# An encoder layer on one core: where the bias lines are drawn, and how the norm's gain g reaches all partitions

## The chip, the cores and the metric

The kernel runs on one core of a Trainium2 chip. A core has five engines with a queue of instructions each: TensorE (PE in the profile, with its weight loads as PEld), VectorE (DVE), ScalarE (ACT), GpSimd (POOL) and SyncE (SP). They run side by side and meet through semaphores; transfers between device memory and the on-chip buffer are issued from the queues of SP, ACT and POOL and run on 16 shared DMA engines. The metric is the device time of one execution in microseconds, as the median of three runs.

## The reference

An encoder layer on two inputs, a prompt of 256 rows and a sample of 1024 rows, both 1024 wide. Every row is normalised and scaled by a gain, projected, run through two kinds of banded attention, gated, added back, and put through a squared-ReLU MLP. What the change touches is the first norm and the attention's bias:

```python
def _rmsnorm(x, g):
    y = x32 * lax.rsqrt(jnp.mean(x32 * x32, axis=-1, keepdims=True) + RMS_EPS)
    return (y * g.astype(jnp.float32)).astype(x.dtype)
...
    h = _rmsnorm(x, g_mix)
    z = h @ w_in
...
    bias = bias_table.astype(jnp.float32)[_rel_bucket(rel * dist_scale)]
    logits = jnp.where(valid[None, :, None, None], s + bias, NEG_INF)
```

The bias of a head depends on the distance of key and query alone, so that all of it is in one line for each head and each spacing. There are 20 heads and 2048 positions in all such lines together.

## The kernel before

The ten row tiles (128 rows each, eight of the sample and two of the prompt, called tiles 0 to 9 here) stay on chip. Matrix products are made in three TensorE passes on operands that are split into a high and a low part (`hhi`/`hlo` of the rows, `vhi`/`vlo` of weights); later stages use a fast matrix product of seven block products. The order of the first stage is written by hand: each engine's instructions stand in its queue in the order in which the code is written, and every engine takes them strictly from its own queue.

The first stage makes the transposed normalised rows and the value projection. Its steps:

- `load_x(t)` brings tile t, `load_v(v, i)` a piece of the value weights (`vraw`), all on SP's queue. SP also issues `tab` (the bias table), `bg` (the gate's bias, a rearranged load of single elements) and `nsink`, and before the change `gm`, the gain g broadcast from device memory to 128 partitions.
- `square(t)` is ACT's: the sum of squares of tile t, and its square root. `scale(t)` is DVE's: the reciprocal, and tile x reciprocal x `gm` into `xn`.
- `turn(t)` is in steps: eight TensorE transposes of `xn` (tile `tr`), then four copies on ACT to `hhi` and four subtractions on DVE to `hlo`.
- `split_v` makes `vhi` on ACT and `vlo` on DVE (one of four on POOL).
- `values(t, v, ps)` is 24 matmuls of 512 (or 384) columns: the value projection of tile t. `evac` copies it out and stores it.
- `warm(n)` are n matmuls of the identity with itself in fp32, whose result nobody reads; they stand ahead of and between the first transposes.
- `draw(i)` makes 512 positions of all bias lines: a matmul of the one-hot matrix `hot` (33 rows: 32 buckets and one for "outside the window") with the table `tab`, which is split into `tab_hi` and `tab_lo`, so two matmuls; ACT copies the result and POOL stores it to `scr_l`. The four draws stand behind the value projections of tiles 3 to 6. Each needs `hot` rounded to `hr` by POOL, and POOL also issues that load.

A word on transfers. Each transfer adds 16 to one of eight counters when it has landed (for SP and ACT together they are named DMAHW0 to DMAHW7). The counters are given out in turn, in the order in which the kernel's text issues transfers, and a transfer that takes a counter waits in its engine's queue until the one that had it before has landed.

Of the kernel before, what the change touches and what calls it, by code (L numbers as in the profile page):

```python
# [10 lines left out]
F32 = mybir.dt.float32  # L11
F32R = mybir.dt.float32r
AF = mybir.ActivationFunctionType
ALU = mybir.AluOpType

P = 128
D = 1024
# [6 lines left out]
AH = 8  # L24
BH = 4
FF = 4 * D
EPS = 1e-6
NEG = -1e30
BUCKETS, MAXD = 32, 1024
# [68 lines left out]
def encoder_kernel(  # L98
# [5 lines left out]
    nc = tc.nc  # L104
    PSUM = bass.MemoryType.PSUM

    def x_rows(t):
        return x_sample[0, P * t : P * (t + 1), :] if t < 8 else x_prompt[0, P * (t - 8) : P * (t - 7), :]
# [11 lines left out]
    const = ctx.enter_context(tc.tile_pool(name="const", bufs=1))  # L120
# [6 lines left out]
    def slot(name, shape=(P, D), dt=F32):  # L127
        return slots.tile(list(shape), dt, name=name, tag="m", bufs=N_M)
# [7 lines left out]
    def bank(tag, name=None):  # L136
        return psum.tile([P, 512], F32, name=name or tag, tag=tag, bufs={"mm": 3, "sc": 2, "pt": 2, "pv": 1}[tag])
# [111 lines left out]
    nc.vector.memset(eps, EPS)  # L249
    bg = const.tile([P, 2 * KC], F32, name="bg")  # L250
    nsink = const.tile([P, AH], F32, name="nsink")
    tab = const.tile([BUCKETS + 1, AH + 3 * BH], F32, name="tab")
    tab_hi, tab_lo = (const.tile([BUCKETS + 1, AH + 3 * BH], F32R, name=x) for x in ("tab_hi", "tab_lo"))

    nm_b = const.tile([P, ROWS], F32, name="nm_b")
    l_b = const.tile([P, ROWS], F32, name="l_b")
# [19 lines left out]
    NH = AH + 3 * BH  # L276
# [16 lines left out]
    NL = sum(x[5] for x in LINES)  # L293
    scr_l = dram.tile([NH, NL], F32, name="scr_l")
# [378 lines left out]
    with ExitStack() as pre:  # L673
        late = pre.enter_context(tc.tile_pool(name="values", bufs=1))

        def own(name, shape, dt=F32, n=1):
            return late.tile(list(shape), dt, name=name, tag=name, bufs=n)

        xs, sds = {}, {}
        gm = slot("gm")  # L680
# [3 lines left out]
        def load_x(t):  # L684
            xs[t] = slot("xt")
            nc.sync.dma_start(xs[t], x_rows(t))
# [11 lines left out]
        def split_v(v, i, eng=nc.vector):  # L698
            if v == 0:
                hi, lo = wslot("vhi", (P, 2, 512), F32R), wslot("vlo", (P, 2, 512), F32R)  # L700
            else:
                hi, lo = own("v2", (P, 2, 384), F32R, 8), own("v2", (P, 2, 384), F32R, 8)
            src = v_raw.pop((v, i))
            nc.scalar.activation(hi, src, AF.Copy)
            eng.tensor_tensor(lo, src, hi.bitcast(F32), op=ALU.subtract)
            v_parts[v, i] = hi, lo

        def warm(n):
            ps = bank("mm", "warm")
            for _ in range(n):  # L710
                nc.tensor.matmul(ps[:, :P], ident, ident, start=True, stop=True, skip_group_check=True)

        hots = {}

        def load_hot(i):
            if i < NL // 512:
                hs = own("hs", (P, 512))[: BUCKETS + 1, :]
                nc.gpsimd.dma_start(hs, hot[:, 512 * i : 512 * i + 512])
                hots[i] = own("hr", (P, 512), F32R)[: BUCKETS + 1, :]
                nc.gpsimd.tensor_copy(hots[i], hs)  # L720

        def draw(i):

            ps = bank("pv", "line")
            hs = hots.pop(i)
            for k, x in enumerate((tab_lo, tab_hi)):
                nc.tensor.matmul(ps[:NH, :], x, hs, start=not k, stop=k == 1)
            ln = own("vo", (P, 512), n=2)[:NH, :]
            nc.scalar.activation(ln, ps[:NH, :], AF.Copy)
            nc.gpsimd.dma_start(scr_l[:, 512 * i : 512 * i + 512], ln)  # L730
            load_hot(i + 1)

        def square(t):
            xn[t] = slot("xn")
            ss = small.tile([P, 1], F32, name="ss")
            nc.scalar.activation(xn[t], xs[t], AF.Square, accum_out=ss)
            sds[t] = small.tile([P, 1], F32, name="sd")
            nc.scalar.activation(sds[t], ss, AF.Sqrt, bias=eps, scale=1.0 / D)

        def scale(t):  # L740
            rs = small.tile([P, 1], F32, name="rs")
            nc.vector.reciprocal(rs, sds.pop(t))
            nc.vector.scalar_tensor_tensor(xn[t], xs.pop(t), rs, gm, op0=ALU.mult, op1=ALU.mult)
# [48 lines left out]
        def values(t, v, ps, ks=range(KC)):  # L792
            n = NV[v]
            for k in ks:
                lh, ll = h_at(k, P * t, P)
                rh, rl = (x[:, k % 2, :] for x in v_parts[v, k // 2])
                for j, (a, b) in enumerate(((lh, rh), (lh, rl), (ll, rh))):
                    nc.tensor.matmul(ps[:, :n], a, b, start=k == 0 and j == 0, stop=k == KC - 1 and j == 2)

        def evac(t, v, ps):  # L800
            rows = slice(P * t, P * t + P)
            vo = own("vo", (P, 512), n=2)[:, : NV[v]]
            if v == 0:
                nc.vector.tensor_copy(vo, ps)
            else:
                nc.scalar.activation(vo, ps[:, : NV[v]], AF.Copy)
            nc.gpsimd.dma_start(scr_v[rows, 512 * v : 512 * v + NV[v]], vo)

        load_x(0)
        nc.sync.dma_start(gm, g_mix[0].partition_broadcast(P))  # L810
        load_x(1)
        for i in range(4):
            load_v(0, i)
        for t in range(2, 6):
            load_x(t)
        nc.sync.dma_start(tab[:BUCKETS, :], rel_bias)
        nc.sync.dma_start(bg, b_gate[0].rearrange("(k p) -> p k", p=P))
        nc.sync.dma_start(nsink, sink[0].partition_broadcast(P))
        load_v(1, 0)
# [6 lines left out]
        load_x(9)  # L826
        first = small.tile([P, 1], F32, name="sd")
        nc.scalar.activation(first, eps, AF.Sqrt)
        warm(15)

        turns = [turn(t) for t in range(NT)]
        square(0)
        scale(0)
        next(turns[0])
        warm(4)
        square(1)
        scale(1)
        next(turns[0])
        split_v(0, 0)
        next(turns[1])  # L840
        warm(2)
        split_v(0, 1)
        next(turns[1])
        split_v(0, 2, nc.gpsimd)
# [12 lines left out]
        next(turns[1], None)  # L857
        square(4)
        next(turns[2], None)
        nc.vector.memset(tab[BUCKETS:, :], NEG)  # L860
        nc.vector.tensor_copy(tab_hi, tab)
        nc.vector.tensor_tensor(tab_lo, tab, tab_hi.bitcast(F32), op=ALU.subtract)
        load_hot(0)
        nc.vector.tensor_scalar(nsink, nsink, -1.0, None, op0=ALU.mult)
        for t in range(2):
            evac(t, 0, pss[t])
# [2 lines left out]
        for t in range(2, NT):  # L869
            if t + 1 < NT:  # L870
                next(turns[t + 1])
                next(turns[t + 1])
            if t + 3 < NT:
                square(t + 3)
            if t + 2 < NT:
                scale(t + 2)
            if t + 1 < NT:
                next(turns[t + 1], None)
            if t < 6:
                split_v(1, t - 2)  # L880
            if t > 7:
                next(b0)
            ps = bank("mm", "v")
            values(t, 0, ps)
            if 3 <= t < 3 + NL // 512:
                draw(t - 3)
            evac(t, 0, ps)

        def more():
# [14 lines left out]
        for t in (4, 5, 6, 7, 8, 9, 0, 1, 2, 3):  # L904
            ps = bank("mm", "v")
# [6 lines left out]
    if True:  # L912
# [16 lines left out]
        class Rows:  # L929
# [15 lines left out]
            def sum(self, t0, n, ps, other):  # L945
                out, a, b = self.views(t0, n, ps, other)
                nc.vector.scalar_tensor_tensor(out, a, self.scale, b, op0=ALU.mult, op1=ALU.add)
# [401 lines left out]
    if True:  # L1349
# [54 lines left out]
        n = len(order)  # L1404
# [87 lines left out]
        for i, (x, b, c) in enumerate(jobs):  # L1492
            t0, n = BLOCKS[b]
# [15 lines left out]
            ps = bank("mm")  # L1509
# [79 lines left out]
    with ExitStack() as pre:  # L1589
# [7 lines left out]
        gm = slot("gm2")  # L1597
# [12 lines left out]
        for hh in range(2):  # L1610
# [17 lines left out]
            for t in range(NT):  # L1628
                m = parts.pop(t)
                ps = bank("mm")  # L1630
# [391 lines left out]
```

## Time and profile before

| | us |
|---|---|
| median of three runs | 1682.21 (1681.28 to 1682.70) |
| the profiled execution | 1681.33 |
| its span on the core | 1679.5 |
| TensorE busy in the span | 1667.2 (99%) |
| VectorE, ScalarE, GpSimd busy | 951.4, 718.2, 512.1 |

The span is the time between the first and the last instruction on the core; 1.8 us of the profiled execution lie around it. Rows of the timeline begin with the start and the duration in us; where a group of equal instructions is merged, "x8" tells how many. Behind "<-" stand in brackets the idle time of the engine just before, and what ended it. TensorE's rows overlap each other, since a matmul starts before the one ahead of it has drained; so its steps are read from start to start. A plain fp32 matmul leaves two records.

### The profile page before, as it was taken

Reading aid. Unit: us, or ns where it says so; the run is one execution under the profiler, and the core shown is the slowest. Engines: PE = TensorE matmul, PEld = TensorE weight load, DVE = VectorE, ACT = ScalarE, POOL = GpSimd, SP = SyncE. Lnnn points to the kernel's source line nnn. Section 1 sums busy time; section 2 is a strip of 40 time slices with the busy share of each in tenths; the row PEclk is TensorE's granted clock in tenths of the full one; section 3 lists DMA queues with packets and bytes.
Section 4 is the critical chain, followed back from the end, with each engine's and each line's share of the span. In section 5 each row is a group of like instructions: output and inputs, shape, how many; then the busy total and the mean of one; then the engine's idle time right before and its main releaser. Section 6 shows DMA issues by size and latency. Waiting matters only on the chain. (4 is left out here: it accounts for less than half of the span.)

```text
span 1679.5 us, 24942 instructions
## 1 busy us (share of the span) xinstructions
PE 1667.2 (99%) x9268; PEld 1414.5 (84%) x9268; DVE 951.4 (57%) x1544; ACT 718.2 (43%) x1485; POOL 512.1 (30%) x404
## 2 busy tenths in 40 slices
PE   9999999999999999999999999999999999999998
PEld 7898888887788888888888888888888888888886
DVE  6732233455563566677278445545556775867665
ACT  6332323356662556654176333333334333333445
POOL 1312222122111463200100556556454250514240
PEclk9999999999999999999999999999999999999999
DMA  7426562567676793845121443443356934733333
GB/s 249 151 58 127 133 133 76 162 192 197 192 198 188 184 262 119 296 133 201 38 88 59 160 156 109 136 160 115 125 190 227 363 105 131 256 102 116 120 119 125
DMA packets 225881, 262.45 MB, mean 156 GB/s; under 512 B 30017, under 2 KB 154737, under 8 KB 225761
## 3 DMA queue, kind: packets, MB, share of 16 engines
q1 hardware_dynamic: 217536, 239.80, 44.8%
q0 software_dynamic: 7936, 20.54, 5.6%
q8 instruction: 73, 1.20, 0.3%
q10 hardware_dynamic: 288, 0.52, 0.1%
q14 instruction: 48, 0.39, 0.1%
HBM read 175.13 MB, written 90.92 MB: 158 GB/s over the span
## 5 line engine op out<-in xcount | busy, mean ns | idle before, releaser
L347 PE MATMUL dn<-dhi,ulo 128*128 128x512 f32 x448 | 174.5, 389 | 0.2
L347 PE MATMUL dn<-dlo,uhi 128*128 128x512 f32 x448 | 174.3, 389 | 0.0
L347 PE MATMUL dn<-dhi,uhi 128*128 128x512 f32 x448 | 174.3, 389 | 0.0
L347 PE MATMUL x<-chi,wlo 128*128 128x512 f32 x424 | 167.0, 394 | 0.1
L347 PE MATMUL x<-clo,whi 128*128 128x512 f32 x424 | 165.7, 391 | 0.1
L347 PE MATMUL x<-chi,whi 128*128 128x512 f32 x424 | 165.1, 389 | 0.0
L314 DVE TENSOR_TENSOR wlo<-ta,whi 128x1024 fp32r<-128x1024 f32 x30 | 55.2, 1841 | 173.8 <-ACT whi L312 173.8
L314 DVE TENSOR_TENSOR wlo<-raw,whi 128x1024 fp32r<-128x1024 f32 x60 | 89.0, 1483 | 98.1 <-ACT whi L312 96.5
L393 POOL TENSOR_TENSOR tb<-raw 128x512 f32<-128x512 f32 x25 | 32.5, 1298 | 366.8 <-DMA raw<-in_w_in_dram 146.5
L347 PEld LDWEIGHTS dn<-dhi,ulo 128*128 128x128 f32 x448 | 84.1, 188 | 18.4 <-PE dn L347 0.5
L347 PEld LDWEIGHTS dn<-dlo,uhi 128*128 128x128 f32 x448 | 84.1, 188 | 17.5
L347 PEld LDWEIGHTS dn<-dhi,uhi 128*128 128x128 f32 x448 | 84.1, 188 | 17.4
L347 PEld LDWEIGHTS x<-chi,whi 128*128 128x128 f32 x424 | 79.6, 188 | 17.0
L347 PEld LDWEIGHTS x<-chi,wlo 128*128 128x128 f32 x424 | 79.8, 188 | 15.7 <-ACT c L1936 0.6
L347 PEld LDWEIGHTS x<-clo,whi 128*128 128x128 f32 x424 | 79.8, 188 | 14.9 <-DVE clo L314 0.4
L1716 POOL TENSOR_TENSOR t<-raw,t 128x1024 f32<-128x1024 f32 x16 | 45.0, 2828 | 154.3 <-DMA raw<-in_w_down_dram 154.3
L186 DVE TENSOR_TENSOR ulo<-uraw,uhi 128x1024 fp32r<-128x1024 f32 x56 | 88.7, 1606 | 3.5 <-ACT uhi L185 3.5
L1865 DVE TENSOR_TENSOR v<-v,dn 128x512 f32<-128x512 f32 x90 | 59.4, 682 | 41.2 <-PE dn L347 36.6
L1965 POOL TENSOR_TENSOR u<-u,u 128x640 f32<-128x640 f32 x16 | 25.1, 1570 | 171.7 <-ACT u L1883 171.7
L186 DVE TENSOR_TENSOR dlo<-raw,dhi 128x1024 fp32r<-128x1024 f32 x32 | 48.6, 1540 | 47.2 <-ACT dhi L185 46.3
L347 PE MATMUL dn<-dhi,up 128*128 128x512 f32 x224 | 73.5, 389 | 0.0
L185 ACT ACTIVATE dhi<-raw 128x1024 fp32r<-128x1024 f32 x32 | 33.5, 1058 | 93.5 <-PE dn L347 93.0
(325 smaller groups left out, 4690.6 us busy)
## 6 DMA issues: line engine op xcount, KB each, us to landing
scr_u<-u SPq DMA_DIRECT2D x112, 320.0 KB, 2.6
uraw<-scr_u SPq DMA_DIRECT2D x56, 512.0 KB, 4.5
raw<-in_w_down_dram SPq DMA_DIRECT2D x36, 512.0 KB, 6.2
raw<-in_w_up_dram SPq DMA_DIRECT2D x32, 512.0 KB, 5.4
raw<-in_w_in_dram SPq DMA_DIRECT2D x25, 512.0 KB, 5.4
sg<-scr_g SPq DMA_DIRECT2D x32, 256.0 KB, 6.3
uraw<-scr_u SPq DMA_DIRECT2D x28, 256.0 KB, 4.3
v<-scr_v SPq DMA_DIRECT2D x96, 64.0 KB, 2.8
```

What stands on the lines that cost most here:

```text
L185: nc.scalar.activation(hi, src, AF.Copy)
L186: nc.vector.tensor_tensor(lo, src, hi.bitcast(F32), op=ALU.subtract)
L314: nc.vector.tensor_tensor(lo, src, hi.bitcast(F32), op=ALU.subtract)
L347: nc.tensor.matmul(ps, a, b, start=first and i == 0, stop=last and i == len(seq) - 1, skip_group_check=True)
L393: (nc.vector if vector else nc.gpsimd).tensor_tensor(o, x, y, op=ALU.subtract)
L1716: nc.gpsimd.tensor_tensor(o, a, b, op=ALU.subtract)
L1865: nc.vector.tensor_tensor(v, v, ps, op=ALU.add)
L1965: nc.gpsimd.tensor_tensor(u[S1], u21, u22, op=ALU.add)
```

## The change

Two things are moved, and one is added.

1. `gm` isn't broadcast by a transfer any more. SP's first transfer brings g as one row of 4 KB (`g_row`), TensorE multiplies it by a row of ones (two fp32 matmuls of 512 columns, ahead of the last `warm`), and DVE copies the two results to `gm`.
2. The bias lines are drawn in plain fp32 and in one accumulation: `tab` is a table padded with zeros in which draw j is shifted by 32 columns, so that the four draws fill rows 0, 32, 64 and 96 of one PSUM bank. Draw 0 stands between the transposes of tiles 0 and 1, draws 1 to 3 behind those of tile 1, in the place of `warm(4)` and `warm(2)`. The eight matmuls behind tiles 3 to 6 go, as do the split of the table on DVE, the rounding of `hot` on POOL and its loads there. One copy of the whole bank on ACT stands behind the values of tile 3, with four stores.
3. `tab` and the two halves of `hot` (33 rows of 1024 numbers, 132 KB each) are issued from ACT's queue: `tab` first of all, `hot` between the `square` of tile 0 and that of tile 1.

```diff
+        pads = NL // 512
+        edge = 32 * (pads - 1)
+        tab = own("tab", (P, edge + P))[: BUCKETS + 1, :]
+        nc.vector.memset(tab, 0.0)
+        nc.vector.memset(tab[BUCKETS:, edge : edge + NH], NEG)
+        nc.scalar.dma_start(tab[:BUCKETS, edge : edge + NH], rel_bias)
+        hots = []
+        drawn = bank("pv", "line")
...
+            hots.append(slot("hot")[: BUCKETS + 1, :])
+            nc.scalar.dma_start(hots[i], hot[:, D * i : D * i + D])
+
+        def draw(j):
+
+            nc.tensor.matmul(drawn, tab[:, edge - 32 * j : edge - 32 * j + P],
+                             hots[j // 2][:, 512 * (j % 2) : 512 * (j % 2) + 512], start=not j, stop=j == pads - 1)
+
+        def store_lines():
+
+            ln = own("vo", (P, 512), n=2)
+            nc.scalar.activation(ln, drawn, AF.Copy)
+            for j in range(pads):
+                nc.gpsimd.dma_start(scr_l[:, 512 * j : 512 * j + 512], ln[32 * j : 32 * j + NH, :])
...
+        ones = own("ones", (P, P))[:1, :]
+        nc.vector.memset(ones, 1.0)
+        g_row = slot("g_row")[:1, :]
+        nc.sync.dma_start(g_row, g_mix)
         load_x(0)
-        nc.sync.dma_start(gm, g_mix[0].partition_broadcast(P))
         load_x(1)
...
         for t in range(2, 6):
             load_x(t)
-        nc.sync.dma_start(tab[:BUCKETS, :], rel_bias)
         nc.sync.dma_start(bg, b_gate[0].rearrange("(k p) -> p k", p=P))
...
-        warm(15)
+        warm(8)
+        for h in range(2):
+            ps = bank("mm", "g")
+            nc.tensor.matmul(ps, ones, g_row[:, 512 * h : 512 * h + 512], start=True, stop=True)
+            nc.vector.tensor_copy(gm[:, 512 * h : 512 * h + 512], ps)
+        warm(10)
 
         turns = [turn(t) for t in range(NT)]
         square(0)
+        load_hot(0)
+        load_hot(1)
         scale(0)
         next(turns[0])
-        warm(4)
+        draw(0)
         square(1)
         scale(1)
         next(turns[0])
         split_v(0, 0)
         next(turns[1])
-        warm(2)
+        for j in (1, 2, 3):
+            draw(j)
...
-            if 3 <= t < 3 + NL // 512:
-                draw(t - 3)
+            if t == 3:
+                store_lines()
             evac(t, 0, ps)
```

In the order of the built program, ACT's queue from its start stood so before (the names are those above; what an instruction waits for stands in brackets, where DMAHW0 to 7 are the counters of transfers):

```order
L828 ACT_TABLE_LOAD
L828 ACTIVATE sd<-eps 128x1 [waits DVE_49]
L736 ACTIVATE xn,ss<-xt 128x1024 [waits DMAHW0_49]
L738 ACTIVATE sd<-ss,eps 128x1 [waits Activation_49]
L736 ACTIVATE xn,ss<-xt 128x1024 [waits DMAHW2_49]
L738 ACTIVATE sd<-ss,eps 128x1 [waits Activation_49]
L769 ACTIVATE hhi<-tr 128x2x128 [waits PE_49]
```

and now:

```order
L716 DMA tab<-in_rel_bias_dram 32x20 [waits DVE_49]
L833 ACT_TABLE_LOAD
L833 ACTIVATE sd<-eps 128x1
L739 ACTIVATE xn,ss<-xt 128x1024 [waits DMAHW2_49]
L741 ACTIVATE sd<-ss,eps 128x1 [waits Activation_49]
L722 DMA hot<-in_hot_dram 33x1024 [waits DMAHW2_49]
L722 DMA hot<-in_hot_dram 33x1024 [waits DMAHW3_49]
L739 ACTIVATE xn,ss<-xt 128x1024
L741 ACTIVATE sd<-ss,eps 128x1 [waits Activation_49]
L772 ACTIVATE hhi<-tr 128x2x128 [waits PE_49]
```

Three issues of transfers stand in ACT's queue that weren't there, two of them ahead of tile 1's square, and each of these two waits for a counter. Which transfers had these counters before is seen on SP's queue, which now stands so from the first transfer to tile 7 (the last two `xt` rows are tiles 6 and 7):

```order
L815 DMA g_row<-in_g_mix_dram 1x1024
L684 DMA xt<-in_x_sample_dram 128x1024 x2
L691 DMA vraw<-in_w_in_dram 128x2x512 x4
L684 DMA xt<-in_x_sample_dram 128x1024 [waits DMAHW0_49]
L684 DMA xt<-in_x_sample_dram 128x1024 [waits DMAHW1_49]
L684 DMA xt<-in_x_sample_dram 128x1024 [waits DMAHW2_49]
L684 DMA xt<-in_x_sample_dram 128x1024 [waits DMAHW3_49]
L822 DMA bg<-in_b_gate_dram 128x16x1 [waits DMAHW4_49]
...
L684 DMA xt<-in_x_sample_dram 128x1024 [waits DMAHW2_49]
L684 DMA xt<-in_x_sample_dram 128x1024 [waits DMAHW3_49]
```

So counter 2 is taken by tile 0, then by tile 4, then by tile 6; counter 3 by tiles 1, 5 and 7. In the kernel's text `load_hot` is called behind `load_x(9)`, and the two halves of `hot` are the next on counters 2 and 3: their waits are for a count of 48, three landed transfers.

On TensorE's queue the start stood so before:

```order
L711 MATMUL warm<-ident 128x128 x15
L338 MATMUL tr<-ident,xn 128x128 x8
L711 MATMUL warm<-ident 128x128 x4
L338 MATMUL tr<-ident,xn 128x128 x8
L711 MATMUL warm<-ident 128x128 x2
L798 MATMUL v<-vhi,hhi 128x512
```

and now:

```order
L709 MATMUL warm<-ident 128x128 x8
L837 MATMUL g<-g_row,ones 128x512 x2
L709 MATMUL warm<-ident 128x128 x10
L336 MATMUL tr<-ident,xn 128x128 x8
L726 MATMUL line<-hot,tab 128x512
L336 MATMUL tr<-ident,xn 128x128 x8
L726 MATMUL line<-hot,tab 128x512 x3
L801 MATMUL v<-vhi,hhi 128x512
```

The four draws stand ahead of the first matmul of the value projection, and the first of them ahead of tile 1's transposes.

More of the change, by code (lines that the diff above doesn't have):

```diff
@@ L251, in encoder_kernel @@
     nsink = const.tile([P, AH], F32, name="nsink")
-    tab = const.tile([BUCKETS + 1, AH + 3 * BH], F32, name="tab")
-    tab_hi, tab_lo = (const.tile([BUCKETS + 1, AH + 3 * BH], F32R, name=x) for x in ("tab_hi", "tab_lo"))
     nm_b = const.tile([P, ROWS], F32, name="nm_b")
@@ L711, in warm @@
                 nc.tensor.matmul(ps[:, :P], ident, ident, start=True, stop=True, skip_group_check=True)
-        hots = {}
-        def load_hot(i):
[L716 to L731, printed above, removed]
+        pads = NL // 512
[6 more added lines that the diff above has]
+        drawn = bank("pv", "line")
+        def load_hot(i):
+            hots.append(slot("hot")[: BUCKETS + 1, :])
[8 more added lines that the diff above has]
+                nc.gpsimd.dma_start(scr_l[:, 512 * j : 512 * j + 512], ln[32 * j : 32 * j + NH, :])
         def square(t):
@@ L859, in encoder_kernel @@
         next(turns[2], None)
[L860 to L863, printed above, removed]
         nc.vector.tensor_scalar(nsink, nsink, -1.0, None, op0=ALU.mult)
```

## The prediction

> **What bounds the kernel now.** I read the page first, then who TensorE waits for, then the timeline of the first 60 us, the transfers of that stretch, and the order of the built program. The page says which engine sets the time:
>
> ```profile
> span 1679.5 us, 24942 instructions
> PE 1667.2 (99%) x9268; PEld 1414.5 (84%) x9268; DVE 951.4 (57%) x1544; ACT 718.2 (43%) x1485; POOL 512.1 (30%) x404
> ```
>
> A busy TensorE could still be a stalled one, so the waits are needed; these are all that the view of TensorE's waits has:
>
> ```profile
> PE warm L711 <- POOL ident masks.py:199: 1.4, 1, 1.4
> PE tr L338 <- DVE xn L743: 1.2, 2, 0.9
> PE sc L1146 <- DVE m L1148: 1.0, 2, 0.7
> PE v L798 <- DVE vlo L705: 0.7, 1, 0.7
> PE sc L541 <- DMA qk<-scr_kb: 0.5, 1, 0.5
> PE mm L192 <- ACT z L999: 0.2, 1, 0.2
> ```
>
> Five microseconds in all, of which those on `ident`, `xn` and `vlo` belong to the start. From then on TensorE is a solid row of matmuls to the tail. So two things count: when the solid row starts, and how many steps are in it. Whatever delays its start delays the end by as much, for nothing later has slack to give it back. The start, on three engines:
>
> ```profile
> 7.87 1.06 ACT L736 ACTIVATE xn<-xt 128x1024 f32<-128x1024 f32 x1 [1.60 <-DMA xt<-in_x_sample_dram]
> ...
> 9.57 1.28 DVE L743 SCALAR_TENSOR_TENSOR xn<-xt,rs,gm 128x1024 f32<-128x1024 f32 x1
> ...
> 10.91 1.09 PE L338 MATMUL tr<-ident,xn 128*128 128x128 f32 x8 [0.92 <-DVE xn L743]
> ...
> 12.21 0.48 PE L798 MATMUL v<-vhi,hhi 128*128 128x512 f32 x1
> ...
> 13.37 0.50 PE L798 MATMUL v<-vlo,hhi 128*128 128x512 f32 x1 [0.68 <-DVE vlo L705]
> ```
>
> Tile 1's square starts when tile 1 lands (7.87). Its transposes follow 3.04 us later, and the second value matmul, from which the row is solid, 5.50 us later. One matmul was done ahead of it; with steps of 0.23 us the solid row starts, in effect, at 13.14.
>
> **Part 1: the draws leave the solid row.** A seam between two tiles without a draw, and one with:
>
> ```profile
> 31.15 0.40 PE L798 MATMUL v<-vhi,hlo 128*128 128x512 f32 x1
> 31.39 1.04 PE L338 MATMUL tr<-ident,xn 128*128 128x128 f32 x8
> 32.18 0.48 PE L798 MATMUL v<-vhi,hhi 128*128 128x512 f32 x1
> ...
> 37.49 0.39 PE L798 MATMUL v<-vhi,hlo 128*128 128x512 f32 x1
> 37.81 0.41 PE L727 MATMUL line<-hr,tab_lo 33*20 33x512 f32 x1
> 38.06 0.39 PE L727 MATMUL line<-hr,tab_hi 33*20 33x512 f32 x1
> 38.37 1.10 PE L338 MATMUL tr<-ident,xn 128*128 128x128 f32 x8
> 39.23 0.48 PE L798 MATMUL v<-vhi,hhi 128*128 128x512 f32 x1
> ```
>
> From the last value matmul of one tile to the first of the next it is 32.18 - 31.15 = 1.03 us without and 39.23 - 37.49 = 1.74 us with a draw: 0.71 us for each, 2.84 us for four. That is the whole gain to be had here. The table's split on DVE, the rounding on POOL and three of the four copies on ACT go too, but TensorE waits for none of them in this stretch; nor for the one wider copy and its four stores on POOL behind tile 3. They count as nothing, covered by the solid row.
>
> **Part 2: the two issues of `hot` hold ACT.** This decides. In the built program they stand on ACT's queue between tile 0's square and tile 1's, and each waits until a counter of transfers stands at 48, that is until three transfers on it have landed. The third on the one counter is tile 6, on the other tile 7, since `load_hot` is called behind `load_x(9)` in the text. Until tile 7 is there, ACT can't start tile 1's square, nor the copies `hhi` and `vhi`; DVE waits for these, and TensorE for both. The loads themselves wait for nothing that ACT does, so it is no deadlock. How late are tiles 6 and 7? First SP's queue, with a wait that shows how it stands still at such a counter, then the times from issue to landing: of tile 6 from the stretch 20.3 to 20.8, of tile 7 from 21.3 to 22.
>
> ```profile
> SPq L816 <- DMA vraw<-in_w_in_dram: 1.2, 1, 1.2
> ```
>
> ```profile
> 0.74 0.39 SPq L686 DMA_DIRECT2D xt<-in_x_sample_dram  x1
> 1.18 0.42 SPq L810 DMA_DIRECT2D gm<-in_g_mix_dram  x1
> ...
> 12.12 6.25 SPq L818 DMA_DIRECT2D nsink<-in_attn_sink_dram  x1
> ...
> 20.43 0.94 SPq L686 DMA_DIRECT2D xt<-in_x_sample_dram  x2
> ```
>
> ```profile
> xt<-in_x_sample_dram SPq DMA_DIRECT2D x1, 512.0 KB, 5.7
> ```
>
> ```profile
> xt<-in_x_sample_dram SPq DMA_DIRECT2D x1, 512.0 KB, 6.5
> ```
>
> Tile 6 is issued at 20.43 and lands at 26.1. Tile 7 is issued half of the 0.94 later, at 20.90, and lands at 27.4. They are late because 18 transfers stand ahead of them, and because the issue of `nsink` is stuck for 6.25 us behind `bg`. What moves them now: the 512 KB of the broadcast are gone from the queue, at the rate of a full stretch (406 GB/s, below) 0.52 MB or 1.3 us; the row of g goes ahead of tile 0, one issue of 0.42 us later. Net 0.9 us earlier: tile 6 at 25.2, tile 7 at 26.5. Bounds: 27.8 if the broadcast's place is worth nothing, 24.5 if, beyond the 0.9, the stores of values that run beside these loads now and then won't are worth 2 us.
>
> ```profile
> 15.00:16.00 1.00, 1.00 (x7) 0.81 (x6) 1.00 (x4) 1.00 (x2) 1.00 (x1) 1.00 1.02 406
> ```
>
> ```profile
> 1652.69 0.40 ACTq L1835 DMA_DIRECT2D out_dram<-v  x1
> ```
>
> An issue on ACT's queue takes 0.40, so tile 1's square starts at 26.5 + 0.4 = 26.9 instead of 7.87, and tile 1's transposes can start 3.04 us later, at 29.9.
>
> **Part 3: the draws ahead of the first value matmul.** TensorE has nothing to do from about 12 us on, and its clock matters for what follows. The `warm` matmuls show both speeds (the last column of figures is the count of records, two for a call):
>
> ```profile
> 1.36 6.36 PE L711 MATMUL warm<-ident 128*128 128x128 f32 x30 [1.36 <-POOL ident masks.py:199]
> ...
> 8.94 1.06 PE L711 MATMUL warm<-ident 128*128 128x128 f32 x8
> ```
>
> Fifteen calls in 6.36 us from a standing start are 0.42 us for 128 columns; four calls later take 0.265 each. For the 512 columns of a draw that is 1.70 us at the low and at most 1.06 us at the high speed. Though the page's granted clock reads full speed throughout, the standing start is the nearest row for a TensorE that comes out of 16 us of idleness. The Trainium skill, "TensorE: Matmul & The Clock Gate", Part 1, says that an array idle for a window of about 3.4 us falls back to half the clock until it has been busy for about as long; by it nearly all draws go at half speed, three of them in 5.1 us, and the sum below would be 20.6 us, where draws at full speed give 18.7. No row of this profile shows a long idle stretch after the start.
>
> When does draw 0 run? The first half of `hot` is issued at 25.2. The nearest landing is that of a quarter of `hot` before:
>
> ```profile
> hs<-in_hot_dram POOLq DMA_DIRECT2D x1, 66.0 KB, 3.0
> ```
>
> So it lands at about 28.2, and draw 0 runs from there, at the low speed, to 29.9, just as `xn` of tile 1 comes. The second half, issued at 26.5, is there at 29.5, ahead of draws 2 and 3. The eight transposes take 1.09 at speed and up to twice that: 1.5, done at 31.4. The last three draws take between 3.2 and 5.1; I take 4.3, at half speed until about 34: at the start it lasted for some 5.6 us of matmuls, and here it begins with draw 0. The first value matmul starts at 35.7. ACT and DVE are ready before: by the 5.50 us of the first fence at 26.9 + 5.5 = 32.4. So the draws, and no longer `vlo`, are what the solid row waits for last: 35.7 - 13.14 = 22.6 us later.
>
> **Part 4: g by TensorE.** Eight `warm` calls, two fp32 matmuls of 512 columns, two copies on DVE, ten `warm` calls; all of it is over at about 11 us, and what needs it, tile 0's transposes, is read by ACT's `hhi` only after the hold. It costs nothing as long as ACT stands still; its price without that cover is in the first rival. The wait that goes, DVE's 0.21 us for `gm`, is worth nothing either.
>
> **Sum.** 22.6 - 2.8 = 19.8 us later. The profiled execution took 1681.33 us, 0.9 below the median of the runs, so 1701.1 by it and **1702 us** against the median of 1682.2. A difference of 0.2%, 3.4 us, is about what can be told from none here.
>
> **Rival A, not slower: ACT isn't held.** If ACT issued `hot` without standing still, at 6.3 us behind tile 0's square, the rest has to be priced without cover:
>
> ```profile
> 6.67 1.28 DVE L743 SCALAR_TENSOR_TENSOR xn<-xt,rs,gm 128x1024 f32<-128x1024 f32 x1 [0.21 <-DMA gm<-in_g_mix_dram]
> ...
> 8.01 1.09 PE L338 MATMUL tr<-ident,xn 128*128 128x128 f32 x8 [0.29 <-DVE xn L743]
> ```
>
> ```profile
> 24.71 1.27 DVE L804 COPY vo<-v 128x512 f32<-128x512 f32 x2
> ```
>
> Eight `warm` calls at half speed from 1.36 end at 4.75, g's two matmuls at 8.15, ten `warm` calls at full speed at 10.8 (the copies, 0.64 each, and tile 0's scaling, 1.28, end before). Tile 0's transposes start at 10.8 instead of 8.01 and end at 11.9; draw 0 to 12.95, tile 1's transposes to 14.05, three draws at 1.06 to 17.2. The solid row starts 4.1 us later and is 2.8 us shorter: 1683.5, no difference that can be told. It becomes slower by 0.2% once ACT is held to about 10.6 us (10.6 + 3.0 + 1.5 + 4.3 = 19.4, which is 13.14 + 2.84 + 3.4), long before tiles 4 or 5 are there, let alone 6 and 7. For it speaks only that before shows no wait of ACT at an issue; against it that SP's queue does stand still at its own. The same page of the Trainium skill (section "Architectural detail: the array is 16× 32×32, not 1× 128×128") has ACT take its instructions strictly in turn, which is the forecast and not this rival. 9%.
>
> **Rival B, a shorter hold.** Without the broadcast and with `tab` off SP's queue, `nsink` might not get stuck. Then only the rate limits: the 1.8 MB from the second value weights to tile 7, at 406 GB/s 4.5 us behind tile 5. Tile 5 is the last of four issues, at about 7.8, and by the landing in that stretch there at 18.8, now 17.9; so tile 7 at 22.4, 4.1 us sooner: 1698.
>
> ```profile
> 4.79 3.40 SPq L686 DMA_DIRECT2D xt<-in_x_sample_dram  x4
> ```
>
> ```profile
> xt<-in_x_sample_dram SPq DMA_DIRECT2D x1, 512.0 KB, 11.0
> ```
>  Against rival B: `bg`, with its single elements, still stands ahead of `nsink`. 10%.
>
> **Rival C, a longer one.** The halves of `hot` share the engines with the full queue of SP; if they land after 6.5 us, as tile 7 does, instead of 3.0, draws 2 and 3 wait until 33 and the row starts some 2 to 4 us later: 1704 to 1706. 7%.
>
> **Chances.** The forecast has 73%, with its own range of 1698.5 to 1705 from the bounds (tile 7 at 24.5 and matmuls at full speed: 24.5 + 0.4 + 3.04 + 1.09 + 3.2 = 32.2, 16.2 us; tile 7 at 27.8 and matmuls at half speed: 38.5, 22.5 us). B and C widen it to 1694 to 1707. Rival A's 9%, spread over both sides of no change, is what stands for same and faster; a percent more for the unknown.
>
> **What would show it.** ACT idle from about 6 us to the landing of tile 7, ended by a transfer `xt` at an issue of `hot` (26 to 27); TensorE idle from about 11 to 28; `line` ahead of the first `v`, which starts at 35 or 36; no `line` behind tiles 3 to 6, and seams of 1.03 us there; a TensorE row from then on that is the old one, shifted. I am wrong if tile 1's square starts near 8, or if the long idle stretch brings a wait of its own later.

## The result: 1.6% slower, further than the forecast

The changed kernel takes 1709.65 us (median; 1708.18 to 1710.30) against 1681.9 us of the kernel before, timed beside it: a ratio of 1.0163, 95% interval 1.0150 to 1.0177. That is 27.8 us more, where 20 were forecast, and outside the range. The first lines of the changed kernel's page, with the line of the granted clock (the share of TensorE's full clock, in tenths, over 40 equal slices of the span):

```profile
span 1706.4 us, 24923 instructions
PE 1679.4 (98%) x9266; PEld 1421.1 (83%) x9266; DVE 958.5 (56%) x1546; ACT 716.4 (42%) x1482; POOL 510.4 (30%) x396
...
PEclk7999999999999999999999999999999999999999
```

TensorE's share is a point lower and the first slice of its clock reads 7, so the difference should lie in the first slice, 43 us long. The view of TensorE's waits has one new row that is large:

```profile
PE line L726 <- DMA hot<-in_hot_dram: 16.9, 1, 16.9
```

The timeline of the start, in the order in which one waits for the other (`hot` issued from ACT's queue, tile 1's square on ACT, draw 0, tile 1's transposes, three draws, the first values; the brackets hold the idle time ahead and what ended it):

```profile
25.24 1.61 ACTq L722 DMA_DIRECT2D hot<-in_hot_dram  x2
26.90 1.06 ACT L739 ACTIVATE xn<-xt 128x1024 f32<-128x1024 f32 x1 [20.58 <-DMA xt<-in_x_sample_dram]
...
31.32 2.04 PE L726 MATMUL line<-hot,tab 33*128 33x512 f32 x2 [16.85 <-DMA hot<-in_hot_dram]
33.30 1.97 PE L336 MATMUL tr<-ident,xn 128*128 128x128 f32 x8
35.20 5.49 PE L726 MATMUL line<-hot,tab 33*128 33x512 f32 x6
40.61 0.79 PE L801 MATMUL v<-vhi,hhi 128*128 128x512 f32 x1
41.20 0.63 PE L801 MATMUL v<-vlo,hhi 128*128 128x512 f32 x1
...
44.51 0.40 PE L801 MATMUL v<-vhi,hhi 128*128 128x512 f32 x1
44.75 0.39 PE L801 MATMUL v<-vlo,hhi 128*128 128x512 f32 x1
```

ACT stood still for 20.58 us and went on at 26.90, ended by a tile's landing. Draw 0 had to wait for `hot` until 31.32. The first value matmul started at 40.61, and the first nine went at 0.43 us a step instead of 0.23, until 44.51. The tenth value matmul started at 15.30 in the kernel before, so the solid row is 29.2 us late.

What the draws save by leaving the row can be read in the same trace, at the four seams that had one before. Two of them now take 1.02 and 1.03 us, as forecast, the other two 1.34:

```profile
66.72 0.39 PE L801 MATMUL v<-vhi,hlo 128*128 128x512 f32 x1
66.96 1.03 PE L336 MATMUL tr<-ident,xn 128*128 128x128 f32 x8
67.75 0.48 PE L801 MATMUL v<-vhi,hhi 128*128 128x512 f32 x1
...
79.39 0.39 PE L801 MATMUL v<-vhi,hlo 128*128 128x512 f32 x1
79.91 1.06 PE L336 MATMUL tr<-ident,xn 128*128 128x128 f32 x8
80.73 0.48 PE L801 MATMUL v<-vhi,hhi 128*128 128x512 f32 x1
```

So four draws are worth 2.2 us and not 2.84: behind all of these seams the first matmul on the prompt's rows (`phi`) starts at 93.75 instead of 66.75, 27.0 us later, and the span is longer by 26.9. Why two seams grew isn't settled. The clock of the first stretch, in windows of five microseconds (the columns are busy time of TensorE, its weight loads, DVE, ACT and POOL, then the granted clock, the DMA engines' share and GB/s):

```profile
10.00:15.00 5.00, 4.47 (x25) 4.23 (x23) 0.97 (x1) 0.00 (x0) 0.00 (x0) 1.00 1.04 408
15.00:20.00 5.00, 0.00 (x0) 0.00 (x0) 0.00 (x0) 0.00 (x0) 0.00 (x0) 0.71 0.80 178
20.00:25.00 5.00, 0.00 (x0) 0.00 (x0) 0.00 (x0) 0.00 (x0) 0.00 (x0) 0.50 0.91 306
...
35.00:40.00 5.00, 5.00 (x8) 1.83 (x6) 3.63 (x5) 4.77 (x12) 2.35 (x1) 0.50 0.00 0
40.00:45.00 5.00, 5.00 (x13) 3.49 (x13) 3.14 (x5) 1.63 (x5) 0.00 (x0) 0.56 0.02 3
45.00:50.00 5.00, 5.00 (x24) 4.13 (x23) 0.00 (x0) 0.00 (x0) 0.00 (x0) 1.00 0.00 0
```

TensorE stood idle from 14.5 us on and fell to half its clock at 17.1, and it stayed there through all draws and transposes. Two things were then to be settled: whether it is the counters' wait on ACT that costs the most, and why the rest came out 7 us larger than forecast.

### The profile page after: what moved, and what is told of

Read it like the earlier page. It is cut to its first block, busy times and chain, and to the rows that moved or that the text cites. A ratio compares the mean times of both kernels' runs of the same rounds, so it can differ in the third digit from the quotient of the medians.

```text
span 1706.4 us, 24923 instructions
## 1 busy us (share of the span) xinstructions
PE 1679.4 (98%) x9266; PEld 1421.1 (83%) x9266; DVE 958.5 (56%) x1546; ACT 716.4 (42%) x1482; POOL 510.4 (30%) x396
## 4 chain that ended last, share of the span: by engine, by line
PE 94%; DVE 2%; DMA 2%; ACT 1%; SPq 1%; issue 0%; ACTq 0%; DVEq 0%
PE dn L345 22%; PE x L345 19%; PE mm L192 14%; PE z L345 9%; PE v L801 6%; PE y L345 5%; PE mm L345 5%; PE sc L345 3%; PE pv L345 3%; PE pv L1197 2%; PE pt L1181 1%; PE sc L539 1%; PE pv L584 1%; PE pt L571 1%; PE tr L336 1%; PE sc L1155 1%
## 5 line engine op out<-in xcount | busy, mean ns | idle before, releaser
L185 ACT ACTIVATE dhi<-raw 128x1024 fp32r<-128x1024 f32 x32 | 33.5, 1058 | 92.8 <-PE dn L345 92.3
```

## The experiments

### Is it the hold?

One word of the changed kernel is different: `hot` is issued from GpSimd's queue, so that no issue stands between ACT's two squares.

```diff
-            nc.scalar.dma_start(hots[i], hot[:, D * i : D * i + D])
+            nc.gpsimd.dma_start(hots[i], hot[:, D * i : D * i + D])
```

> The changed kernel with one word different: hot is issued from GpSimd's queue, whose counters are its own, so that ACT waits for no counter of tiles 6 and 7. All else, g's matmuls and the four draws ahead of the values, is as changed. Theory of the hold: tile 1's square starts near 8 us again instead of 26.9, and the time falls by the hold, less what TensorE's longer start costs without cover (tile 0's transposes at 13.2 as in the changed kernel, draw 0 to 16.2, tile 1's transposes to 18.0, three draws at half clock to 23.4, values from there at half clock for some 3 us): 9 us over before, about 1691. Rival, the TensorE work is the cost (g and the draws at half clock delay the start by themselves): it stays above 1700.

Measured: 1683.04 us against 1681.32, a ratio of 1.0013 (1.0004 to 1.0022). Without the hold 1.7 us of the 27.8 are left, which the interval just tells from none:

```profile
6.20 1.06 ACT L739 ACTIVATE xn<-xt 128x1024 f32<-128x1024 f32 x1
...
13.21 1.53 PE L336 MATMUL tr<-ident,xn 128*128 128x128 f32 x8
14.67 1.12 PE L726 MATMUL line<-hot,tab 33*128 33x512 f32 x2
...
16.75 2.84 PE L726 MATMUL line<-hot,tab 33*128 33x512 f32 x6
...
19.52 0.50 PE L801 MATMUL v<-vhi,hhi 128*128 128x512 f32 x1
```

Tile 1's square starts at 6.20. The draws take 0.43 a record, half of what they take in the changed kernel, so that the first values start at 19.5 and not at the 23.4 of the expectation, and at once at full rate. That is 6.4 us later than before for 2.2 us saved. The profiled execution is the longest of ten (1686.66 us) and shows most of that loss; the shorter ones have no trace.

Two more kernels move the end of the hold without changing queues. In the first, tile 0's square and the two issues stand ahead of the loads of tiles 6 and 7 in the text, so that the counters are those of tiles 4 and 5; the order on ACT's and on SP's queue stays.

```diff
...
+        square(0)
+        load_hot(0)
+        load_hot(1)
         load_x(6)
...
-        square(0)
-        load_hot(0)
-        load_hot(1)
```

> The changed kernel with tile 0's square and the two issues of hot ahead of the loads of tiles 6 and 7 in the text; every queue's order stays. The issues then wait for tiles 4 and 5 instead of 6 and 7. Theory of the hold: it ends when tile 5 lands, near 17 or 18 instead of 26.5, and the time falls by as much, 8 to 9 us, to 1701. If what holds ACT is something else (the queue of transfers as a whole, or nsink): no change.

Measured: 1694.93 us, a ratio of 1.0086 (1.0071 to 1.0101). Against the changed kernel's 1.0163 that is 0.0077 of 1681, or 13 us, less, where 8 to 9 were expected.

```profile
15.57 2.00 ACTq L722 DMA_DIRECT2D hot<-in_hot_dram  x2
17.63 1.06 ACT L739 ACTIVATE xn<-xt 128x1024 f32<-128x1024 f32 x1 [11.07 <-DMA xt<-in_x_sample_dram]
18.77 2.04 PE L726 MATMUL line<-hot,tab 33*128 33x512 f32 x2 [8.32 <-DMA hot<-in_hot_dram]
...
28.05 0.79 PE L801 MATMUL v<-vhi,hhi 128*128 128x512 f32 x1
```

The hold ends 9.3 us sooner, as expected. The time falls by more, for draw 0 starts 12.55 us sooner: here `hot` is there 3.2 us after its issue at 15.57, with 71 to 97 GB/s moved between 16 and 19 us, and in the changed kernel 6.1 us after 25.24, with 344 to 404 GB/s moved between 25 and 29. In the second kernel the issues stand ahead of tiles 2 to 5, behind `g_row` and `tab` on their counters:

```diff
...
+        square(0)
+        load_hot(0)
+        load_hot(1)
         for t in range(2, 6):
             load_x(t)
...
```

> As before, but the two issues stand ahead of tiles 2 to 5 in the text, behind tile 0's square on ACT's queue still. Their counters then had g_row and tab, which land early, so ACT doesn't stand still. Theory of the hold: tile 1's square at 6 to 8 us; hot lands some 6 us after its issue at 6.3, before or with tile 0's transposes; time as in the kernel with hot from GpSimd's queue, 1683. Rival, that it is GpSimd's queue that made that kernel fast and an ACT queue with issues in it is slow: above 1695.

Measured: 1687.73 us, 1.0045 (1.0028 to 1.0062). ACT issues at 6.80 and squares tile 1 at once:

```profile
6.80 0.91 ACTq L722 DMA_DIRECT2D hot<-in_hot_dram  x2
7.76 1.06 ACT L739 ACTIVATE xn<-xt 128x1024 f32<-128x1024 f32 x1 [0.67 <-DMA hot<-in_hot_dram]
...
19.60 0.50 PE L801 MATMUL v<-vhi,hhi 128*128 128x512 f32 x1
```

So issues on ACT's queue don't cost the 26 us by themselves; what the counters wait for does. The first values start at 19.60, as with GpSimd's queue, and the profiled execution is no longer than the one there (1685.3 against 1686.66). But the median is more than the 1683 expected, and 5 us above that of GpSimd's queue, with intervals that don't meet: two of the four executions, with a mean granted clock of 0.995, took 1689. They have no trace, and what made them longer stays open.

### What g by TensorE costs

With the hold kept, g's part is undone: broadcast transfer, 15 `warm` calls.

```diff
...
+        nc.sync.dma_start(gm, g_mix[0].partition_broadcast(P))
...
-        warm(8)
-        for h in range(2):
...
-        warm(10)
+        warm(15)
```

> The changed kernel with g's part alone undone: broadcast transfer, 15 warm matmuls, no g by TensorE; hot is still issued from ACT behind the counters of tiles 6 and 7. The forecast had g cost nothing under the hold: then the 512 KB come back ahead of tile 7, the hold ends about 1 us later, and the time is 1710 to 1711. If g by TensorE has a price of its own here, it is below 1707.

Measured: 1710.85 us, 1.0176 (1.0159 to 1.0193): as forecast, no difference that can be told from the changed kernel. The hold ends at 27.47 instead of 26.90. The same without the hold (`hot` from GpSimd's queue):

> The kernel of e1, and g is broadcast by a transfer as before, with 15 warm matmuls and no g by TensorE; the draws stay ahead of the values. If g by TensorE costs nothing, this is e1's time. If it costs its matmuls and keeps TensorE at half clock: tile 0's transposes at 8.0, draws at full clock at 0.95 each, the first value matmul near 14.9, 1.7 later than before with 2.8 us of draws gone: about 1681.

Measured: 1688.01 us, 1.0042 (1.0027 to 1.0057), 7 us more than expected and 5 more than with g by TensorE.

```profile
9.42 1.06 ACT L739 ACTIVATE xn<-xt 128x1024 f32<-128x1024 f32 x1 [3.16 <-DMA xt<-in_x_sample_dram]
...
12.46 1.09 PE L336 MATMUL tr<-ident,xn 128*128 128x128 f32 x8 [2.23 <-DVE xn L746]
...
13.49 5.13 PE L726 MATMUL line<-hot,tab 33*128 33x512 f32 x6
...
18.54 0.80 PE L801 MATMUL v<-vhi,hhi 128*128 128x512 f32 x1
```

With the broadcast and `hot` both ahead of it, tile 1 lands at 9.4; with g by TensorE it was there by 6.2. TensorE idles for 2.2 us, its granted clock falls to 0.5 at 13.9, when the three draws have just begun, and they take 5.13 us instead of the 2.84 of the kernel with g by TensorE. The expectation had them at full clock. The first value matmul still starts 1 us sooner than there (18.54 against 19.52), but 13 go at half clock, and the fourteenth is 1.6 us behind (24.20 against 22.59). So the row instead of the broadcast is worth something once nothing holds ACT, by way of the clock: 1.6 us between the two traces, 5 between the medians.

### Is it the clock that makes the draws long?

Under the hold, 50 more `warm` calls fill the time in which TensorE is idle.

```diff
         next(turns[0])
+        warm(50)
         draw(0)
```

> The changed kernel, hold and all, with 50 more warm matmuls ahead of draw 0, in the stretch in which TensorE has nothing to do. If the clock makes the draws and the first values slow: the draws take 0.95 instead of 1.75 each, the first values go at full rate, and it is some 6 us faster than the changed kernel, 1703. If the draws are slow for another reason, no change from 1709.

Measured: 1711.11 us, 1.0178 (1.0163 to 1.0193), no gain, and the question stays open: the calls ran at full clock and ended at 21.7, and in the 10.9 us that were left the clock fell again, at 25.9.

```profile
10.34 11.33 PE L709 MATMUL warm<-ident 128*128 128x128 f32 x100
...
32.52 2.04 PE L726 MATMUL line<-hot,tab 33*128 33x512 f32 x2 [10.86 <-DMA xt<-in_x_prompt_dram]
```

So the same with 85 calls.

> The changed kernel, hold and all, with 85 more warm matmuls ahead of draw 0 (50 ended 10.9 us before the first half of hot landed, and the clock was at half again by then). If the clock is what makes the draws and the first values slow, and TensorE is busy up to a few us before draw 0: records of the draws at 0.43 to 0.53 instead of 0.87 us, values at 0.23 from the first, the first value matmul near 36 or 37, and 1703 to 1706. If the draws are slow for another reason: no change, 1710.

Measured: 1707.43 us, 1.0160 (1.0138 to 1.0182), and the four executions fall in two pairs: 1703.95 and 1704.15 us with a mean granted clock of 0.999, 1710.71 and 1711.23 with 0.995. The profiled one is of the second pair: its calls ended at 29.6, draw 0 started at 33.5, and in that gap of 3.9 us the clock fell, at 33.0.

```profile
10.46 19.15 PE L709 MATMUL warm<-ident 128*128 128x128 f32 x170
...
33.54 2.04 PE L726 MATMUL line<-hot,tab 33*128 33x512 f32 x2 [3.93 <-DMA hot<-in_hot_dram]
```

The pairs agree with the 6 us that were expected of the clock. No trace was taken of one of the first pair, so that its draws were short is inferred.

Why did the clock stay at half while TensorE was busy with draws? A draw sums over 33 rows of TensorE's array (the "33" in its profile rows), a `warm` matmul over 128. A kernel has the same draws on 128 rows; `hot` is one and `tab` zero in the added rows, so that the sums are the same.

```diff
-        tab = own("tab", (P, edge + P))[: BUCKETS + 1, :]
+        tab = own("tab", (P, edge + P))
...
-            hots.append(slot("hot")[: BUCKETS + 1, :])
-            nc.scalar.dma_start(hots[i], hot[:, D * i : D * i + D])
+            hots.append(slot("hot"))
+            nc.vector.memset(hots[i], 1.0)
+            nc.scalar.dma_start(hots[i][: BUCKETS + 1, :], hot[:, D * i : D * i + D])
```

> The changed kernel with the same four draws on 128 rows instead of 33: tab is zero and hot is one in the rows added, so the sums are the same and a draw streams the same 512 columns. In the changed kernel the clock stayed at half through 9 us of draws and transposes and came back only 3.6 us into the values, which use all 128 rows, as the warm matmuls do. If matmuls on few rows don't count towards the clock: with all rows it comes back during the draws, the first values run at full rate, 2 to 4 us faster, 1706. If it is not the rows (that they are fp32, or the gaps between them): 1709 to 1710.

Measured: 1704.05 us, 1.0142 (1.0127 to 1.0157).

```profile
33.73 2.04 PE L727 MATMUL line<-hot,tab 128*128 128x512 f32 x2 [21.22 <-DMA hot<-in_hot_dram]
35.57 1.92 PE L336 MATMUL tr<-ident,xn 128*128 128x128 f32 x8
37.28 3.81 PE L727 MATMUL line<-hot,tab 128*128 128x512 f32 x6
40.53 0.80 PE L802 MATMUL v<-vhi,hhi 128*128 128x512 f32 x1
41.16 0.40 PE L802 MATMUL v<-vlo,hhi 128*128 128x512 f32 x1
41.40 0.39 PE L802 MATMUL v<-vhi,hlo 128*128 128x512 f32 x1
```

The same number of columns, and the three draws take 3.81 instead of 5.49 us; the granted clock comes back within them, at 39.4, 5.7 us after draw 0's start, and the values step at 0.23 from the second on. By the ratios the kernel is 3.5 us faster than the changed one, with intervals that overlap; in this execution `hot` landed 2.4 us later than in the changed kernel, which hides part of the gain. The traces decide it: in this and the last version below, both with draws on 128 rows, the clock came back within the draws. With 33 rows it never did: in six traces that met the draws at half clock it stayed there for the 9.3 us of draws and transposes (in one of them, the version with two `warm` calls, this is read from the durations), and in a seventh it fell as the three draws began and stayed down to their end.

It wasn't chance in the timing of the clock either. In all eight traces that record a fall and a rise of the granted clock at the start, the two lie a whole multiple of 3.41 us apart: 17.07 and 44.38 in the changed kernel (8 times 3.41), 15.56 and 39.45 here (7 times). If the clock is set anew every 3.41 us, here the stretch from 36.04 to 39.45, full of transposes and draws on 128 rows, brought it up; in the changed kernel neither the stretch from 34.14 to 37.55 nor that from 37.55 to 40.96 did, and TensorE was as busy there, with transposes, draws on 33 rows and one value matmul.

### A version without the hold, tuned

In the kernel with `hot` from GpSimd's queue, tile 0's transposes stood behind ten `warm` calls though their input was there 2 us sooner. With two calls:

```diff
-        warm(10)
+        warm(2)
```

> The kernel with hot from GpSimd's queue (no hold), with 2 instead of 10 warm matmuls behind g's. There the ten ran at half clock until 13.2 and tile 0's transposes stood behind them, though tile 0's scaled rows were there at 11.0. If TensorE's queue is what is late: transposes at 11.0 and the first value matmul 2 us sooner, 1681, level with before. If the warm matmuls are needed for the clock: draws and first values at half clock, 4 to 5 us slower, 1687.

Measured: 1690.49 us, 1.0053 (1.0041 to 1.0066). The transposes start at 11.0 as they should, but all that follows, up to the twelfth value matmul, goes at half speed:

```profile
11.02 1.97 PE L336 MATMUL tr<-ident,xn 128*128 128x128 f32 x8 [1.02 <-DVE xn L746]
...
16.82 5.49 PE L726 MATMUL line<-hot,tab 33*128 33x512 f32 x6
22.24 0.79 PE L801 MATMUL v<-vhi,hhi 128*128 128x512 f32 x1
```

With four calls, and the draws on 128 rows (set to one by GpSimd):

> Hot from GpSimd's queue, 4 instead of 10 warm matmuls behind g's, and the draws on 128 rows (hot is one in the rows added, set by GpSimd ahead of the load, tab is zero there). If rows are what the clock counts, the draws bring it up by themselves and the fewer warm matmuls cost nothing: 1680 to 1682, level with or a little under before. If not: 1685 or more.

Measured: 1683.48 us, 1.0014 (1.0005 to 1.0023), a little above the 1680 to 1682 expected. The clock was at half from 9.3 to 12.7 and came back 1.3 us after draw 0's start. The first values start at 15.95, 3.6 us sooner than with ten calls and 33 rows. The profiled executions differ by nearly that (1683.52 against 1686.66), but the medians don't (1683.48 against 1683.04), since most executions with ten calls were shorter than the profiled one. No version tried beats the kernel before.

## Why the prediction was right or wrong

- **The sign and the hold (part 2): right in the mechanism, lucky in the figure.** Tile 1's square was forecast at 26.9 and started at 26.90. But tiles 6 and 7 were issued 2.0 us sooner than before (the first at 18.46 instead of 20.43) and not 0.9, and took about 1 us longer to land (tile 6 6.8 us instead of 5.7); the two misses cancel. Rival A, that ACT isn't held, fell. With the hold taken away its price of 1683.5 came out at 1683.0, by luck too: the ten `warm` calls ran at half speed until 13.2 there, and the first values start at 19.5 and not at 17.2.
- **The landing of `hot` (part 3): mis-sized, half of the miss.** It was priced at 3.0 us by a load of a quarter of `hot` into a quieter stretch. It took 6.1, in a stretch with 344 to 404 GB/s; that the traffic is the cause rests on the comparison with the 3.2 us of the version held to tile 5. That was rival C, at 7%. Draw 0 started at 31.3 instead of 28.2, and tile 1's transposes 3.4 us later than forecast.
- **The speed of draws, transposes and first values (part 3): the step that failed, the other half.** "At half speed until about 34" took the 5.6 us of half clock at the start, made of matmuls on all rows, as the price for any matmul. Draws on 33 rows left the clock at half for all of their 9.3 us: the transposes took 1.9 instead of 1.5, the three draws 5.4 instead of 4.3, and the first nine value matmuls, which the sum had at full rate, lost 1.9 us more. The page of the Trainium skill that was quoted ("TensorE: Matmul & The Clock Gate", Part 1) has an idle array fall to half the clock after about 3.4 us and come back once it has been busy for about as long. The traces come near it for the fall (2.6 us after the last matmul in the changed kernel) and for the return under values (3.8 us after the first of them), but not under the draws, where TensorE was busy for 9.3 us at 0.50; there the measurement decides.
- **The sum.** 3.4 + 0.4 + 1.1 + 1.9 = 6.8 us over the forecast's 22.6 gives a row that starts 29.4 us late; measured are 29.2. Less 2.2 us for the draws that is 27.0, and the span's difference is 26.9. Either miss alone would have left the time inside the range; its upper end took the landing and the clock as alternatives, and they came together.
- **The draws leaving the solid row (part 1): right in kind, mis-sized.** It is worth 2.2 us instead of 2.84, since two of the four seams take 1.34 us and not 1.03.
- **g by TensorE (part 4): right under the hold** (1710.85 us without it). Without the hold it isn't a cost: the version with the broadcast is 5 us slower by the medians.

## What to carry to other kernels

Before an issue is put on the queue of an engine that computes, find which earlier transfer has the counter it will take: what must land first is set by the place of the call in the text, and the engine stands still until then, whatever the transfer itself needs. A stall of the engine that feeds TensorE can be paid more than once: here TensorE came back at half its clock, and a load that was issued late landed late. Small matmuls put ahead of a dense stage cost by the clock they run at, not by their columns alone.

## What the runs showed of the hardware

- Matmuls on few rows didn't bring TensorE's clock up: 9.3 us of draws on 33 rows and transposes left it at half, in six traces; draws on 128 rows brought it up 5.7 and 1.3 us after the first of them began, in two.
- The granted clock changed in a rhythm: in eight traces its fall at the start and its next rise lie 1 to 10 times 3.41 us apart.
- The granted clock of the windows can't be read at the very start. In the kernel with two `warm` calls the window below says 1.00 while the draws in it run at 0.87 us a record, and full-speed ones take 0.43:

```profile
15.00:20.00 5.00, 5.00 (x12) 2.99 (x13) 3.87 (x7) 4.30 (x8) 1.39 (x1) 1.00 0.78 200
```

  So a mean near 1 is no proof of a fast start. With `hot` on GpSimd's queue the three executions at 0.999 and 1.000 took 1685.4 to 1686.7 us, the seven at 0.998 took 1681.8 to 1683.9.

- The clock fell to half 2.2 to 5.1 us after the last matmul, in the six traces in which TensorE then stood idle for 3.9 us or longer.
- The same 132 KB landed 3.2 us after their issue at 15.6 us, beside 71 to 97 GB/s, and 6.1 us after their issue at 25.2 us, beside 344 to 404 GB/s.
